# A head of the softmax branches in two steps, and the steps in a new order

## The chip, the cores and the metric

One core of one Trainium2 chip runs the whole kernel in one launch. The metric is the device time of the launch in microseconds (us); of the kernel before three runs are known, 1374.14, 1376.45 and 1376.46 us, so the median is 1376.45 us.

## What is computed

Two blocks follow each other, each with two layers, on 512 tokens of width 1024 (batch 1). A layer projects its input, runs four attention branches of four heads each (head width 64), gates each branch, and projects the result back.

```python
# first block, one layer (abridged)
h = x @ w_in                                   # 9 parts
y_mla = causal_softmax(q_nope|rope(q_pe), k_nope|rope(k_pe), v)   # after two rms norms
y_sb  = stick_breaking(sq, sk, sv)             # sigmoid and suffix sums, no softmax
y_fox = causal_softmax(fq, fk, fv, log_decay=cumsum(log_sigmoid(f)))
y_mem = softmax(q @ mk.T) @ mv                 # 256 memory tokens
merged = sum_n sigmoid(merge_r @ w_merge_up)[n] * ((y_n * silu(gate_n)) @ w_branch[n])
x = layer_norm(alpha * x + merged @ w_out)
# second block, one layer (abridged)
z = rmsnorm(x) @ w_in
o_a = dense softmax (2 key heads, normed and rotated)   # 512 x 512 logits
o_b = window softmax with a sink (3 blocks of 128 keys)
o_c = neighbourhood softmax with a bias table
o_d = two softmaxes, (p0 - lam * p1) @ v, then a norm
x = x + concat(o_n * silu(g_n)) @ w_out
```

## The kernel before

All matmuls work on float32 data that is split into a high and a low part (`split`, L319 a cast on ScalarE, L322 a subtraction on VectorE), and each product is three matmuls: high x high, low x high, high x low (`mm3`, L328 to L330). Matmuls are 128 rows by up to 512 columns. A weight unit (128 x 1024 floats, 512 KB) is loaded by SyncE's queue into `raw` and split into `wh` and `wl`; `w_get` keeps the loads three units ahead of the use (`WP = 3`), in the order that the word lists `WEIGHTS1` and `WEIGHTS2` give.

A softmax head works on four query blocks of 128. For each block two or three matmuls write the logits into a PSUM tile `s` (3 of them in rotation). `softmax` then takes the row maximum on VectorE (L525 with a mask, L528 without) and the exponential with its sum on ScalarE (L534), which writes a tile `p`. When the four tiles `p` are there, `av` transposes them on TensorE, 128 x 128 each, into a PSUM tile `T` (L551, 2 tiles in rotation), splits `T` into `th` and `tl`, and multiplies by V into a PSUM tile `O` (L557, L558, one tile). `o_evac` (L585, L586) brings `O` to SBUF. After the second head of a pair `finish` notes the pair; `do_finish` later repeats the reciprocal sums over the columns by four transposes (`rep`, L626, also a `T` tile) and multiplies on VectorE (L640).

Each branch is a Python generator, and a `yield` ends a step. `weave` takes the steps in the order of a word list: `ORDER1` for the layers of the first block, `ORDER2` for those of the second (a number repeats a word, `f` is one `do_finish`). Projections for the gates (`g`), the stick-breaking heads (`sb`) and the other branches (`mem`, `fox`, `mla`; `a`, `b`, `c`, `d`) are the words. The place in this program order is an instruction's priority: a list scheduler then orders each engine's instructions, taking the earliest that its own plan has ready, so neighbouring steps interleave. After the weave of a first-block layer comes `merge`, after any layer the output projection `w_out`.

Buffers that matter here: `p` has 4, 4, 4 and 2 tiles for the four query blocks in the first block and 2 of each in the second; two PSUM tiles for projections (`proj`, `projv`, `projqr`, `projn` share them), three for `s`, two for `T`, one for `O`. In `mla` the key and value step makes V by two `projv` tiles (L424, taken to SBUF by L414 and L415), then the rotary part of the queries, `projqr` (L968), in the same two tiles.

Of the kernel before, what the change touches and what calls it, by code (L numbers as in the profile page):

```python
# [66 lines left out]
mq:0 mq:1 sb:0 sb:256 gz:6 sbv:0 sbv:1 sbv:2 gz:7 gz:2 gz:3 m:0 m:1 mk:0 mk:1 mv:0 mv:1 sb:128 sb:384 fox:0  # L67
fox:256 cq:0 cq:1 cq:2 gz:4 ckv:0 gz:5 ckv:1 foxv:0 foxv:1 gz:0 fox:128 fox:384 gz:1 kvb qr qb mr mu:0 wb:0
# [3 lines left out]
qa:0 qa:1 ka qd:0 qd:1 kd qc:0 vd g2:6 g2:7 g2:0 g2:1 vab:0 vab:1 g2:2 g2:3 qb2:0 g2:4 kc:0 qb2:1 kb g2:5 vc:0  # L72
# [222 lines left out]
ORDER1 = "first sb g sb g misc sb g2 mem3 fox mem sb2 fox mem mla2 sb g2 mla g mla f fox mla f2 sb fox2 g2 fox g mla f fox mla g fox mla f2 mla f mla3 f"  # L295
ORDER2 = "a d3 c d2 g2 d g2 a g d g f a g b a g f a c b2 a b2 g c g f c d c2 f2 b c f b c f2 w2"
# [14 lines left out]
class Build:  # L311
# [522 lines left out]
    def memory(self, l):  # L834
        self.mem_kv(l)
        yield
        for pr in range(2):
            o, sm = self.new_o(), self.sums()
            for e in range(2):
                h = 2 * pr + e  # L840
                P = []
                for i in range(4):
                    s = self.qk(self.qm[pr][e], self.mks[h], self.mkl[h], i, 0, 256)
                    P.append(self.softmax(i, s, 256, sm[:, e, i : i + 1]))
                self.av(P, [(0, 256)] * 4, lambda j: self.mV[:, j, h], o, e)
# [71 lines left out]
    def mla(self, l):  # L917
# [51 lines left out]
        qr = self.tmp("qr")  # L969
# [6 lines left out]
        for pr in range(2):  # L976
# [14 lines left out]
            for e in range(2):  # L991
                (qa, qb), (ka, kb) = T["q", e], T["k", e]
                P = []
                for i, (_, w) in enumerate(CAUSAL):
# [3 lines left out]
                    P.append(self.softmax(i, s, w, sm[:, e, i : i + 1], self.c["causal"][:, S - w :], sscale=sc))  # L998
                self.av(P, CAUSAL, lambda j: V[pr][:, j, e], o, e)
# [67 lines left out]
    def fox(self, l):  # L1067
# [3 lines left out]
        for pr in range(2):  # L1071
# [10 lines left out]
            for e in range(2):  # L1082
                P = []
                for i, (_, w) in enumerate(CAUSAL):
                    s = self.qk(q[e], ks[e], k2[e], i, 0, w, q2[e], 68)
                    P.append(self.softmax(i, s, w, sm[:, e, i : i + 1], self.c["causal"][:, S - w :]))
                self.av(P, CAUSAL, lambda j: V[pr][:, j, e], o, e)
# [196 lines left out]
    def dense_a(self, l):  # L1284
# [25 lines left out]
        for pr in range(2):  # L1310
            o, sm = self.new_o(), self.sums()
            for e in range(2):
                P = []
                for i in range(4):
                    s = self.qk(raw[pr][e], ks[pr], kl[pr], i, 0, S)
                    P.append(self.softmax(i, s, S, sm[:, e, i : i + 1], sscale=(qsc[:, i, pr, e : e + 1],)))
                self.av(P, DENSE, lambda j: V[0][:, j, pr], o, e)
# [4 lines left out]
    def window_b(self, l):  # L1322
# [15 lines left out]
        for pr in range(2):  # L1338
            o, sm, nm = self.new_o(), self.sums(), self.sums()
            for e in range(2):  # L1340
                P = []
                top = self.nsink[:, l, 2 * pr + e : 2 * pr + e + 1]
                for i, (k0, w) in enumerate(BAND):
                    s = self.qk(q[pr][e], ks[pr], kl[pr], i, k0, w)
                    m = band[:, (128, 0, 0, 0)[i] :][:, :w]
                    P.append(self.softmax(i, s, w, sm[:, e, i : i + 1], m, nm=nm[:, e, i : i + 1], top=top))
                self.av(P, BAND, lambda j: self.vb[:, j, pr], o, e)
# [8 lines left out]
    def diff_d(self, l):  # L1356
# [34 lines left out]
        for pr in range(2):  # L1391
            ku = [unit(hl[2], cols(2 * pr + c, 32), (0, 1, 0, 1)) for c in range(2)]
            o, sm = self.new_o(), self.sums()
            for e in range(2):
                qu = [unit(hl[pr], cols(2 * e + c, 32), (0, 0, 1, 1)) for c in range(2)]
                P = []
                for i in range(4):
# [11 lines left out]
                    P.append(p)  # L1409
                self.av(P, DENSE, lambda j: V[:, j, pr], o, e)  # L1410
# [75 lines left out]
```

## Time and profile before

| | us |
|---|---|
| median of 3 runs | 1376.45 |
| the profiled execution, its own time | 1373.97 |
| its span, first to last instruction | 1372.2 |
| TensorE busy in the span | 1338.4 |
| VectorE busy | 1002.0 |
| ScalarE busy | 816.4 |

The span is 1.8 us shorter than the execution's own time. In the trace the weaves lie at about 15 to 297 us, 410 to 690 us, 803 to 1040 us and 1092 to 1328 us; `merge` follows the first two (to about 345 and 740 us). A matmul's recorded duration is longer than its distance to the next one, since matmuls are pipelined, so a wait that is shorter than that overlap does not show as idle time; the number in brackets at a row's end is idle time and names the instruction that ended it. PEclk is the granted share of TensorE's clock: 1.00 is 2.4 GHz, 0.50 is 1.2 GHz.

### The profile page before, as it was taken

To read this page: it belongs to the slowest core of one execution; us is meant where nothing else is said; L and a number is where in the kernel's file an instruction comes from. 1 tells how busy PE (TensorE), PEld (TensorE's weight loads), DVE (VectorE), ACT (ScalarE), POOL (GpSimd) and SP (SyncE) were. 2 spreads that over 40 slices of the span, in tenths; PEclk is the share of its full clock that TensorE was granted. 3 is DMA by queue.
4 is the path that set the end of the run, shared out by engine and by line. 5 is a ranking of instruction groups with operands and counts; after the bars stand their busy time and mean duration, and the time that the engine had idled before them with its cause. 6 is when DMAs were issued, how large, how long until landed. Compare 5 with 4: busy or idle time off the path is not lost.

```text
span 1372.2 us, 20002 instructions
## 1 busy us (share of the span) xinstructions
PE 1338.4 (98%) x7096; PEld 1099.4 (80%) x7096; DVE 1002.0 (73%) x2075; ACT 816.4 (59%) x1662; POOL 4.3 (0%) x12
## 2 busy tenths in 40 slices
PE   8999999999999999999999999999999999999998
PEld 7887787777789877887777898887877888878776
DVE  6666655998854666476989876788877576888885
ACT  4584556766413755467756344776965446678763
POOL 0000000000000000000000000000000000000000
PEclk9999999999999999999999999999999999999999
DMA  7544223243525434224236345413444265225241
GB/s 232 173 128 106 87 68 93 77 123 114 176 78 152 135 93 137 62 65 108 89 100 190 118 126 153 137 51 104 127 125 156 102 177 154 65 67 146 73 136 70
DMA packets 62419, 160.32 MB, mean 117 GB/s; under 512 B 11184, under 2 KB 11824, under 8 KB 62320
## 3 DMA queue, kind: packets, MB, share of 16 engines
q1 hardware_dynamic: 62320, 159.05, 39.1%
q8 instruction: 56, 0.92, 0.3%
q14 instruction: 43, 0.35, 0.1%
HBM read 117.92 MB, written 8.91 MB: 92 GB/s over the span
## 4 chain that ended last, share of the span: by engine, by line
PE 80%; DVE 8%; ACT 7%; DMA 2%; issue 2%; SPq 0%; DVEq 0%; ACTq 0%
PE proj L328 11%; PE proj L329 11%; PE proj L330 11%; PE T L551 4%; PE pso L330 3%; PE pso L329 3%; PE pso L328 3%; PE O L557 2%; PE O L558 2%; PE projwb L329 2%; PE projwb L328 2%; PE projwb L330 2%; PE s L512 2%; DMA raw<-in_w_dram 2%; PE s L513 2%
## 5 line engine op out<-in xcount | busy, mean ns | idle before, releaser
L328 PE MATMUL proj<-zth,wh 128*128 128x512 f32 (+1 forms) x864 | 322.9, 374 | 7.4 <-ACT wh L319 5.4
L330 PE MATMUL proj<-zth,wl 128*128 128x512 f32 (+1 forms) x864 | 322.7, 374 | 0.0
L329 PE MATMUL proj<-ztl,wh 128*128 128x512 f32 (+1 forms) x864 | 321.9, 373 | 0.3
L322 DVE TENSOR_TENSOR wl<-raw,wh 128x1024 fp32r<-128x1024 f32 (+2 forms) x153 | 182.8, 1195 | 113.3 <-ACT wh L319 111.4
L319 ACT CAST wh<-raw 128x1024 fp32r<-128x1024 f32 (+2 forms) x153 | 157.8, 1031 | 147.5 <-PE proj L329 119.4
L328 PEld LDWEIGHTS proj<-zth,wh 128*128 128x128 f32 x864 | 164.0, 190 | 30.5 <-ACT wh L319 5.4
L330 PEld LDWEIGHTS proj<-zth,wl 128*128 128x128 f32 x864 | 164.0, 190 | 24.7 <-DVE wl L322 1.0
L329 PEld LDWEIGHTS proj<-ztl,wh 128*128 128x128 f32 x864 | 164.2, 190 | 22.8 <-DVE ztl L322 0.8
L322 DVE TENSOR_TENSOR tl<-T,th 128x512 fp32r<-128x512 f32 (+3 forms) x176 | 99.6, 576 | 33.0 <-ACT th L319 31.6
L319 ACT CAST th<-T 128x512 fp32r<-128x512 f32 (+3 forms) x176 | 86.0, 498 | 55.9 <-PE T L551 45.5
L551 PE MATMUL T<-ct,p 128*128 128x128 f32 x560 | 87.3, 275 | 2.7 <-DVE o L640 1.7
L528 DVE TENSOR_REDUCE nm<-s 128x1 f32<-128x512 f32 (+1 forms) x128 | 77.8, 614 | 14.4 <-PE s L513 9.0
L551 PEld LDWEIGHTS T<-ct,p 128*128 128x128 f32 x560 | 66.3, 140 | 19.2 <-DVE o L640 2.6
L534 ACT ACTIVATE p<-s,nm 128x512 f32<-128x512 f32 (+1 forms) x96 | 59.1, 618 | 25.4 <-DVE nm L528 24.9
L557 PE MATMUL O<-tl,V 128*128 128x512 f32 (+3 forms) x160 | 60.0, 376 | 1.5 <-DVE tl L322 1.1
L558 PE MATMUL O<-th,V 128*128 128x512 f32 (+3 forms) x160 | 55.3, 349 | 0.0
L329 PE MATMUL projv<-wl,zth 128*128 128x256 f32 (+1 forms) x192 | 54.7, 285 | 0.0
L328 PE MATMUL projv<-wh,zth 128*128 128x256 f32 (+1 forms) x192 | 54.6, 284 | 0.0
L330 PE MATMUL projv<-wh,ztl 128*128 128x256 f32 (+1 forms) x192 | 54.4, 283 | 0.0
L1107 ACT ACTIVATE sg<-projmu 128x512 f32<-128x512 f32 x64 | 38.1, 598 | 22.7 <-DVE sg L1114 11.6
L330 PE MATMUL projwb<-y,wl 128*128 128x512 f32 x128 | 51.0, 401 | 0.0
L328 PE MATMUL projwb<-y,wh 128*128 128x512 f32 x128 | 51.0, 401 | 0.0
(378 smaller groups left out, 2898.8 us busy)
## 6 DMA issues: line engine op xcount, KB each, us to landing
raw<-in_w_dram SPq DMA_DIRECT2D x173, 512.0 KB, 4.1
xs<-y SPq DMA_DIRECT2D x12, 512.0 KB
ks<-hs SPq DMA_DIRECT2D x32, 128.0 KB, 2.6
early<-xs SPq DMA_DIRECT2D x16, 256.0 KB, 5.1
bias<-in_bias_dram SPq DMA_DIRECT2D x8, 448.0 KB, 4.5
qs<-hs SPq DMA_DIRECT2D x24, 128.0 KB, 3.3
qs<-ls SPq DMA_DIRECT2D x24, 128.0 KB, 2.7
hs<-ls SPq DMA_DIRECT2D x24, 128.0 KB, 2.2
```

The source lines that it names most:

```text
L319: self.nc.scalar.copy(h, src)
L322: self.nc.vector.tensor_tensor(l, src, h, ALU.subtract)
L328: self.nc.tensor.matmul(ps, ah, bh, start=i == 0, stop=False)
L329: self.nc.tensor.matmul(ps, ah, bl, start=False, stop=False)
L330: self.nc.tensor.matmul(ps, al, bh, start=False, stop=i == n - 1)
L512: self.nc.tensor.matmul(s, q[:, cols(i)], k[:, k0 : k0 + w], start=True, stop=False)
L528: nc.vector.tensor_reduce(nm, s, AX.X, ALU.max, negate=True)
L534: nc.scalar.activation(p[:, :w], src, AF.Exp, bias=nm, scale=sc, accum_out=sm)
L551: nc.tensor.transpose(T[:, cols(a)], P[i][:, c : c + 128], self.ident)
L557: nc.tensor.matmul(o, vsel(j), tl[:, :w], start=j == 0, stop=False, skip_group_check=True)
L558: nc.tensor.matmul(o, vsel(j), th[:, :w], start=False, stop=j == nk - 1, skip_group_check=True)
L1107: a = nc.scalar.activation(sg, ps, AF.Sigmoid)
```

## The change

A `yield` is put between the logits-and-exponentials part and the `av` part of a head in all seven softmax branches (in `neigh_c` also one behind the first head), so a head is two steps. `ORDER1`, `ORDER2`, `WEIGHTS1` and `WEIGHTS2` are new lists over the finer steps. No instruction that computes is added or taken away; on every engine the counts by operation, output and shape are equal in both programs.

```diff
-mq:0 mq:1 sb:0 sb:256 gz:6 sbv:0 sbv:1 sbv:2 gz:7 gz:2 gz:3 m:0 m:1 mk:0 mk:1 mv:0 mv:1 sb:128 sb:384 fox:0
+mq:0 mq:1 sb:0 gz:6 sb:256 sbv:0 sbv:1 sbv:2 gz:7 gz:2 gz:3 m:0 m:1 mk:0 mk:1 mv:0 mv:1 sb:128 sb:384 fox:0
...
-ORDER1 = "first sb g sb g misc sb g2 mem3 fox mem sb2 fox mem mla2 sb g2 mla g mla f fox mla f2 sb fox2 g2 fox g mla f fox mla g fox mla f2 mla f mla3 f"
-ORDER2 = "a d3 c d2 g2 d g2 a g d g f a g b a g f a c b2 a b2 g c g f c d c2 f2 b c f b c f2 w2"
+ORDER1 = "first g sb2 misc sb g3 mem6 sb mem sb fox mem g fox sb mem f g mla2 g mla2 fox mla sb f2 fox5 f fox3 g2 mla g mla f mla fox f mla g mla3 f mla4 f"
+ORDER2 = "a d3 c a d2 g2 d2 g d g3 d2 g2 a2 f b a3 b a2 f c b a b g c b2 c d b c2 f c g c2 f d f b3 f c2 b c2 f w c f w"
...
                     P.append(self.softmax(i, s, w, sm[:, e, i : i + 1], self.c["causal"][:, S - w :], sscale=sc))
+                yield
                 self.av(P, CAUSAL, lambda j: V[pr][:, j, e], o, e)
...
+                yield
                 self.av32(P, V[e], O, e)
+                if e == 0:
+                    yield
```

Three places of TensorE's order follow. The first is the key and value step of `mla` in a first-block layer: `projv` makes V, `projqr` takes the PSUM tile of the first `projv`, and `s` are logits of a fox head. Before:

```order
L329 MATMUL projv<-wl,ckh 128x256
L330 MATMUL projv<-wh,ckl 128x256
L512 MATMUL s<-hs 128x128
L513 MATMUL s<-ls 128x128
L512 MATMUL s<-hs 128x256
L513 MATMUL s<-ls 128x256
L328 MATMUL projqr<-cqh,wh 128x512
```

and now, from the end of the first `projv` tile on (the last row is the first of the second tile's twelve; behind those come four more `O` matmuls, then `projqr`):

```order
L330 MATMUL projv<-wh,ckl 128x256
L557 MATMUL O<-tl,V 128x512
L558 MATMUL O<-th,V 128x512
L551 MATMUL T<-ct,p 128x128
L557 MATMUL O<-tl,V 128x384
L558 MATMUL O<-th,V 128x384
L551 MATMUL T<-ct,p 128x128 x2
L328 MATMUL projv<-wh,ckh 128x256
```

The products of a fox head moved between the two tiles of V. The second place is `window_b` in a second-block layer, where the logits of its first head (`s<-ks,hs`) and of its second (`s<-ks,qs`) follow each other. Before:

```order
L512 MATMUL s<-ks,hs 128x384
L513 MATMUL s<-ks,hs 128x384
L512 MATMUL s<-ks,hs 128x256
L513 MATMUL s<-ks,hs 128x256
L512 MATMUL s<-ks,qs 128x256
L513 MATMUL s<-ks,qs 128x256
L512 MATMUL s<-ks,qs 128x384
L1282 MATMUL statd<-ct,sqd 128x2 x4
```

and now:

```order
L513 MATMUL s<-ks,qs 128x256
L328 MATMUL proj<-zth,wh 128x512
L329 MATMUL proj<-ztl,wh 128x512
L330 MATMUL proj<-zth,wl 128x512
L557 MATMUL O<-tl,V 128x512
L558 MATMUL O<-th,V 128x512
L551 MATMUL T<-ct,p 128x128 x2
L557 MATMUL O<-tl,V 128x512
L558 MATMUL O<-th,V 128x512
L551 MATMUL T<-ct,p 128x128 x6
L512 MATMUL s<-ks,qs 128x384
```

Three projection matmuls, four products and eight transposes of another head moved in between the second head's first and second query block. The third place is the first stick-breaking head of a first-block layer; `krt` are four transposes for the rotary keys, and `s` the head's logits. Before, behind a projection:

```order
L328 MATMUL proj<-zth,wh 128x512
L329 MATMUL proj<-ztl,wh 128x512
L330 MATMUL proj<-zth,wl 128x512
L1016 MATMUL krt<-ct,mt 32x128 x4
L890 MATMUL s<-hs 128x128
```

and now, straight behind the stick-breaking values:

```order
L328 MATMUL projv<-wh,zth 128x292
L329 MATMUL projv<-wl,zth 128x292
L330 MATMUL projv<-wh,ztl 128x292
L1018 MATMUL krt<-ct,mt 32x128 x3
L891 MATMUL s<-hs 128x128
```

The logits moved ahead of one projection, so one projection more lies between them and the next matmul of that head.

## Rows read from the trace of the kernel before

**Rows 1.** The page, busy us by engine, share of the span, instructions.

```profile
PE 1338.4 (98%) x7096; PEld 1099.4 (80%) x7096; DVE 1002.0 (73%) x2075; ACT 816.4 (59%) x1662; POOL 4.3 (0%) x12
```

**Rows 2.** Windows of 50 us: length, then busy us of PE, PEld, DVE, ACT, POOL.

```profile
core 0: us, PE busy (x) PEld busy (x) DVE busy (x) ACT busy (x) POOL busy (x), PEclk, DMA share, GB/s
...
200.00:250.00 50.00, 47.77 (x245) 37.66 (x243) 34.83 (x83) 33.95 (x75) 0.00 (x0) 1.00 0.30 84
250.00:300.00 50.00, 48.43 (x256) 37.77 (x256) 47.79 (x122) 39.79 (x90) 0.00 (x0) 1.00 0.32 93
...
600.00:650.00 50.00, 47.41 (x238) 37.42 (x238) 33.42 (x80) 33.01 (x71) 0.00 (x0) 0.97 0.36 96
...
1000.00:1050.00 50.00, 47.84 (x250) 38.65 (x248) 41.16 (x94) 32.67 (x78) 0.00 (x0) 0.97 0.41 122
...
1250.00:1300.00 50.00, 48.05 (x268) 40.18 (x267) 39.90 (x106) 41.53 (x107) 1.05 (x2) 0.97 0.38 104
```

**Rows 3.** Timeline around `projqr`, both layers: start, us, engine, line, idle before.

```profile
231.95 1.28 ACT L614 ACT_TABLE_LOAD   x1
...
234.83 0.65 ACT L414 CAST V<-projv 128x256 fp32r<-128x256 f32 x2
...
235.24 0.76 DVE L415 TENSOR_TENSOR V<-projv,V 128x256 fp32r<-128x256 f32 x2 [0.31 <-ACT V L414]
...
235.80 0.48 PE L328 MATMUL projqr<-cqh,wh 128*128 128x512 f32 x1 [1.37 <-DVE V L415]
...
626.91 0.47 PE L328 MATMUL projqr<-cqh,wh 128*128 128x512 f32 x1 [1.34 <-DVE V L415]
```

**Rows 4.** Timeline of PE behind the second of these waits.

```profile
627.22 0.40 PE L329 MATMUL projqr<-cql,wh 128*128 128x512 f32 x1
627.45 0.40 PE L330 MATMUL projqr<-cqh,wl 128*128 128x512 f32 x1
...
628.56 0.63 PE L328 MATMUL projqr<-cqh,wh 128*128 128x512 f32 x1
628.99 0.63 PE L329 MATMUL projqr<-cql,wh 128*128 128x512 f32 x1
```

**Rows 5.** Timeline of `window_b`, DVE and PE, both layers.

```profile
1002.68 1.22 DVE L322 TENSOR_TENSOR wl<-raw,wh 128x1024 fp32r<-128x1024 f32 x1
...
1004.65 0.62 DVE L525 CUSTOM_DVE_ANT_0 p<-s,band,nsink 128x384 f32<-128x384 f32 x1
...
1003.10 0.28 PE L513 MATMUL s<-ks,qs 128*128 128x256 f32 x1
1005.33 0.44 PE L512 MATMUL s<-ks,qs 128*128 128x384 f32 x1 [1.94 <-DVE sums L525]
...
1292.97 0.45 PE L512 MATMUL s<-ks,qs 128*128 128x384 f32 x1 [1.95 <-DVE sums L525]
```

**Rows 6.** Timeline of the first stick-breaking head, both layers.

```profile
63.50 0.44 PE L907 MATMUL s<-sp,tri 128*128 128x128 f32 x2 [0.57 <-DVE sp L322]
...
452.37 1.21 DVE L322 TENSOR_TENSOR wl<-raw,wh 128x1024 fp32r<-128x1024 f32 x1
...
454.67 0.44 PE L907 MATMUL s<-sp,tri 128*128 128x128 f32 x2 [1.29 <-DVE sp L322]
```

**Rows 7.** Timeline of PE, transposes and products of a fox head behind `projn`.

```profile
243.75 0.33 PE L513 MATMUL s<-kr,qr 68*128 68x384 f32 x1
244.45 0.50 PE L557 MATMUL O<-tl,V 128*128 128x512 f32 x1 [0.37 <-DVE tl L322]
...
245.98 0.27 PE L551 MATMUL T<-ct,p 128*128 128x128 f32 x1
246.44 0.39 PE L557 MATMUL O<-tl,V 128*128 128x256 f32 x1 [0.19 <-DVE tl L322]
```

**Rows 8.** Timeline of PE, transposes that wait for a `T` tile.

```profile
268.14 0.63 PE L551 MATMUL T<-ct,p 128*128 128x128 f32 x4 [0.26 <-DVE o L640]
...
277.06 0.55 PE L551 MATMUL T<-ct,p 128*128 128x128 f32 x3 [0.57 <-DVE o L640]
```

**Rows 9.** TensorE's waits: line, releaser, us in total, times, longest.

```profile
PE proj L328 <- ACT wh L319: 5.4, 1, 5.4
```

More of the change, by code (lines that the diff above doesn't have):

```diff
@@ L66 @@
 WEIGHTS1 = """
-mq:0 mq:1 sb:0 sb:256 gz:6 sbv:0 sbv:1 sbv:2 gz:7 gz:2 gz:3 m:0 m:1 mk:0 mk:1 mv:0 mv:1 sb:128 sb:384 fox:0
-fox:256 cq:0 cq:1 cq:2 gz:4 ckv:0 gz:5 ckv:1 foxv:0 foxv:1 gz:0 fox:128 fox:384 gz:1 kvb qr qb mr mu:0 wb:0
+mq:0 mq:1 sb:0 gz:6 sb:256 sbv:0 sbv:1 sbv:2 gz:7 gz:2 gz:3 m:0 m:1 mk:0 mk:1 mv:0 mv:1 sb:128 sb:384 fox:0
+fox:256 gz:4 cq:0 cq:1 cq:2 gz:5 ckv:0 ckv:1 foxv:0 foxv:1 fox:128 fox:384 gz:0 kvb qr gz:1 qb mr mu:0 wb:0
 wb:1 mu:1 wb:2 wb:3 mu:2 wb:4 wb:5 mu:3 wb:6 wb:7 wo:0 wo:1 wo:2 wo:3 wo:4 wo:5 wo:6 wo:7
@@ L71 @@
 WEIGHTS2 = """
-qa:0 qa:1 ka qd:0 qd:1 kd qc:0 vd g2:6 g2:7 g2:0 g2:1 vab:0 vab:1 g2:2 g2:3 qb2:0 g2:4 kc:0 qb2:1 kb g2:5 vc:0
+qa:0 qa:1 ka qd:0 qd:1 kd qc:0 vab:0 vab:1 vd g2:6 g2:7 g2:0 g2:1 g2:2 g2:3 g2:4 qb2:0 qb2:1 kc:0 kb g2:5 vc:0
 qc:1 kc:1 vc:1 we:0 we:1 wo2:0 wo2:1 wo2:2 wo2:3 wo2:4 wo2:5
@@ L1316, in dense_a @@
                     P.append(self.softmax(i, s, S, sm[:, e, i : i + 1], sscale=(qsc[:, i, pr, e : e + 1],)))
+                yield
                 self.av(P, DENSE, lambda j: V[0][:, j, pr], o, e)
@@ L1346, in window_b @@
                     P.append(self.softmax(i, s, w, sm[:, e, i : i + 1], m, nm=nm[:, e, i : i + 1], top=top))
+                yield
                 self.av(P, BAND, lambda j: self.vb[:, j, pr], o, e)
@@ L1409, in diff_d @@
                     P.append(p)
+                yield
                 self.av(P, DENSE, lambda j: V[:, j, pr], o, e)
@@ L1455, in neigh_c @@
                     P.append(self.softmax(i, s, w, sm[:, e, i : i + 1], bias[:, b0 : b0 + w]))
+                yield
                 self.av32(P, V[e], O, e)
+                if e == 0:
+                    yield
             self.nc.scalar.copy(cr(o), rc(O))
```

## The prediction, made before the changed kernel was run

> **What bounds the kernel now.** I read the page's engine row first: TensorE is busy for 1338.4 of 1372.2 us, VectorE for 1002.0 [rows 1]. TensorE bounds the kernel, and the change gives it the same matmuls; time can come only from its waits and from its clock. The idle time is 1372.2 - 1338.4 = 33.8 us. Then I read the windows of 50 us for two things: where the granted clock is below 1.00 (three windows inside the weaves, at 0.97), and whether another engine is full (VectorE with 47.79 of 50 us at 250 to 300 us, after only 34.83 in the 50 us before) [rows 2]. Last I read the timeline at TensorE's largest waits. They sit where the program order had nothing to put between a result and its use, and they come twice, once in each layer of a block [rows 3, 5 to 8].
>
> **What the clock costs.** Behind the wait of 1.34 us at 626.91 the matmuls of 512 columns start 628.99 - 628.56 = 0.43 us apart, against 627.45 - 627.22 = 0.23 us before [rows 4]: the lower of the two levels, 1.2 against 2.4 GHz. A window at 0.97 lacks 0.03 of 50 us, that is 1.5 us of full clock [rows 2]; by the distances, a stretch at half clock that lacks this much is 3 us long and loses 3 x (1 - 0.23 / 0.43) = 1.4 us. I take 1.5 us for each of the three falls. The equally long wait at 235.80 had no such fall in its window, which stands at 1.00 [rows 2, 3], so a wait of this size takes the clock down in some cases and not in others.
>
> **The change part by part.** Five places, each on TensorE's path.
>
> *A. `projqr`.* It waits for VectorE to take the first V tile out of PSUM, and VectorE waits for ScalarE, which is loading an activation table for 1.28 us and copying gates. Between the second V tile and `projqr` stand only four short matmuls. This costs 1.37 + 1.34 us of idle [rows 3] and one clock fall, 1.5: 4.2 us. Now the products of a fox head stand between the two V tiles and behind the second. The first place of the order shows seven of these rows between the tiles; with the second tile's twelve matmuls (half the columns, so near half of 0.23 us each, 1.4 us) and the products the first tile has about 3 us, where it had under 2. The wait was 1.37 us, so the added 1 us alone would leave a third; but in ScalarE's new order the table load stands behind the casts of V, not ahead of them. Bounds: 0 gained if the wait only shifts, 4.2 if it goes. I take 4.2, since the clock fall needs the long wait.
>
> *B. `window_b`.* The logits of the first head and of the second stand without filler, while only three `s` tiles rotate; the next one waits for a maximum (0.62 us) which is itself late, because VectorE was in a weight split of 1.22 us and another add. Idle 1.94 + 1.95 us [rows 5], and both are in windows at 0.97, so two clock falls, 3.0 us: 6.9 us. In the new order three projection matmuls (0.69 us), four products and eight transposes stand at this point, more than 2 us of TensorE work, and the wait was 1.94. Bounds 0 and 6.9; I take 6.9. If VectorE is late with something else, the cover is gone and the loss returns in full.
>
> *C. The first stick-breaking head.* The matmul with `tri` needs `sp`, which stood on VectorE behind a weight split of 1.21 us; it was late by 0.57 and 1.29 us [rows 6]. Before, 18 projection matmuls stood between the head's logits and `tri`; now 26 stand there, since the projection that came ahead of the logits follows them (the third place of the order). Eight more are 8 x 0.23 = 1.8 us of cover, more than either wait: 1.9 us gained. Bounds 0 and 1.9.
>
> *D. Transposes and products without filler.* From the last logits matmul at 243.75 (384 columns, three quarters of 0.23 us) to the product at 244.45 it is 0.70 us, so 0.53 is lost; at 246.44, behind one transpose of at most 0.1 us, another 0.35 [rows 7]. Twice, for the two layers: 1.8 us, of which the profile shows only 2 x (0.37 + 0.19) as idle. The same fox products now stand beside V (the first place), so I count the 1.8 as gained, bounds 0 and 1.8.
>
> *E. What becomes worse.* `rep` takes one of the two `T` tiles until VectorE has multiplied with it. Before, transposes waited for this 0.26 and 0.57 us in a layer [rows 8]. In the new order I count four places in the kernel where two groups of transposes follow a `rep` with at most two matmuls between, one in `mla` in each first-block layer and one in `window_b` in each second-block layer. At (0.26 + 0.57) / 2 = 0.4 us each this adds 1.7 us; bounds 0 and 4 x 0.57 = 2.3.
>
> *F. What an order does not show.* A to D were chosen because they were the worst. The new order will have a bad place of its own, which depends on how late VectorE and ScalarE run. The nearest row is B: 1.95 + 1.5 = 3.5 us. I take one such place; the bounds are 0 and four of them, 14 us.
>
> At no cost: the weight units and gates that are moved. Their loads follow the same word order as their uses and stay three units ahead, no weight load is among the waits above, and DMA is at 0.41 of its time or less in the windows that I read [rows 2]. The exponentials, splits and `unit` moves of a head are the same in number; their queues are passed in a new order, which is priced with F.
>
> **The sum.** -4.2 - 6.9 - 1.9 - 1.8 + 1.7 + 3.5 = -9.6 us. Against the profiled execution's 1373.97, whose span is 1372.2 and keeps its 1.8 us around it, this is 1364.4 us. That execution lies 2.5 us below the median of the three runs, 1376.45, and just under the fastest, 1374.14; I add half of that distance, so all times below stand against 1375.2. The forecast is 1365.5 us, 0.8% under the median.
>
> **A rule on the clock.** The windows from 200 to 300 us hold many waits of a few tenths and two over half a microsecond, and the clock stays at 1.00 [rows 2, 3, 7, 8]; it fell behind three of the long ones. The Trainium skill ("TensorE: Matmul & The Clock Gate", section "A second HAM failure mode: psum-queue depth-cycling") tells of a kernel that cycled through PSUM banks and whose many micro-idles between groups of matmuls were enough to make the clock go down and up. By that rule the finer interleaving would lose clock where it trades a long wait for many short ones; this trace so far speaks against it, since its finest mixture kept the full clock. The third rival is what it would do here.
>
> **The rivals.**
>
> *1. No change (14%).* VectorE is full at 250 to 300 us, 47.79 of 50 [rows 2]. If that stretch is set by VectorE, cover won before it is only waited for later, in both layers of the first block, and A, C and D come back. B's 6.9 less E and F, 5.2, leaves -1.7 us: 1373.5 us. Against it: TensorE is busy for 48.43 us of that same window, so at most 1.6 us are to be had or lost there by idle time, and VectorE has 15 us free in the window before, where the fox products now go.
>
> *2. Slower: `p` tiles (10%).* A head that is cut holds four `p` tiles from its first step to its second. In the second block there are two of each, and I read from `ORDER2` one point in a layer where three heads are open (`b`, `c`, then `d`). There the third head's maxima and exponentials wait for the first one's transposes, the three `s` tiles stay full, and TensorE runs out of logits. Price: as in B, 3.5 us a place with its clock fall. Two such places, one in each layer, cost 7 and still leave a gain of 2.6. From three places on (9.6 / 3.5 = 2.7) the kernel is slower, from four on by more than can be missed; with six, 21 - 9.6 = +11.4 us: 1386.5 us. For it: the heads are 56, so six is few. Against it: the scheduler lets other work pass, and I find only one such point in a layer.
>
> *3. Slower: the clock (4%).* If many short waits took the clock down in each of the four weaves three times, 12 x 1.5 = 18 us would stand against 9.6 gained: 1383.5 us.
>
> *4. A larger gain (12%).* A to D hold 2.7 + 3.9 + 1.9 + 1.1 = 9.6 us of the 33.8 idle. If the new order also halves the rest, 12 us, and E and F don't come, the gain is 14.8 + 12 = 27 us: 1348 us. For it: cover grows in general when a head is cut. Against it: 5.4 us of the rest is the wait for the first weights, which is not changed [rows 9].
>
> **How the numbers follow.** The forecast holds 60%: a gain of 4 to 18 us, 1357 to 1371 us. A measurement of this kernel tells about 0.2%, 2.8 us, from no change. Faster by more: the forecast and rival 4, 0.60 + 0.12 = 0.72, and I add nothing from the others. Within 0.2%: rival 1, 0.14. Slower: rivals 2 and 3, 0.14. The range for 8 in 10 takes in rival 4, down to 1347, and above, F at its upper bound (10.5 us more) with only a quarter of B gained (5.2 us less): 1381 us.
>
> **What would show it.** Right: no wait over 1 us at `projqr`, at `window_b`'s logits and at the first `tri`; no window of a weave under 1.00; TensorE's idle time near 25 us, with its busy time the same but for the clock. Wrong in A, B or C: the same row still with its wait and its releaser on VectorE. Wrong in F: more than one new wait near 2 us in TensorE's list of waits, and a window at 0.97 behind it. Rival 2: VectorE or ScalarE idle for transposes in the second block. If the clock is at 1.00 throughout and the time is still not below 1371 us, my account of TensorE's waits was wrong as such.

## The result, and the profile after

The changed kernel takes 1360.13 us (median of 4 runs, 1359.7 to 1361.17) against 1376.45 us for the kernel before: a ratio of 0.9882, 95% interval 0.9863 to 0.9901, which is 16.3 us or 1.2% faster. The forecast was 1365.5 us. Part of the 16.3 is the clock: ten runs of the kernel before, timed beside the experiments below, had the mean granted clock that the four of the kernel after had, 0.997 to 0.998, and took 1372.25 to 1374.39 us, about 13 us more than those four. The profiled executions have spans of 1372.2 and 1358.2 us, 14.0 us apart; what follows accounts for these 14.0.

The page's engine row of the kernel after answers to [rows 1]:

```profile
PE 1328.5 (98%) x7096; PEld 1096.4 (81%) x7096; DVE 1000.3 (74%) x2075; ACT 811.3 (60%) x1662; POOL 4.4 (0%) x12
```

The instructions are the same in number. TensorE's idle time went from 33.8 to 1358.2 - 1328.5 = 29.7 us, only 4.1 us less. Its *busy* time fell by 9.9 us for the same 7096 matmuls. So most of the gain stands in time that a list of waits does not show.

TensorE's list of waits after (line, releaser, us in total, times, longest):

```profile
PE proj L328 <- ACT wh L319: 5.6, 1, 5.6
PE projn L328 <- DVE ml L985: 2.6, 2, 1.3
PE pso L328 <- ACT wout L319: 1.7, 2, 1.1
PE s L908 <- DVE sp L322: 1.3, 2, 0.7
...
PE T L551 <- DVE o L640: 1.2, 2, 0.6
PE krt L1018 <- ACT mt L880: 1.1, 2, 0.6
...
PE T L551 <- DVE o L638: 0.6, 2, 0.3
...
PE O L557 <- DVE tl L322: 0.2, 1, 0.2
```

Three of its rows before, for comparison:

```profile
PE T L551 <- DVE o L640: 1.7, 4, 0.6
PE O L557 <- DVE tl L322: 1.1, 4, 0.4
...
PE projn L328 <- DVE ml L984: 0.5, 2, 0.3
```

The waits of `projqr` [rows 3] and of `window_b`'s logits [rows 5] are gone. Three waits are new: `pso` for `wout`, `krt` for `mt`, and `tri` of the second stick-breaking head instead of the first [rows 6]. The wait of `projn` for `ml` has grown from 0.5 to 2.6 us.

The windows of 50 us that answer to [rows 2] (length, busy us of PE, PEld, DVE, ACT, POOL, granted clock, DMA share, GB/s):

```profile
200.00:250.00 50.00, 47.70 (x251) 38.24 (x251) 39.12 (x91) 35.33 (x82) 0.00 (x0) 0.99 0.33 88
250.00:300.00 50.00, 49.50 (x258) 40.06 (x257) 46.67 (x116) 38.53 (x84) 0.00 (x0) 0.98 0.33 95
600.00:650.00 50.00, 47.79 (x263) 38.59 (x262) 41.09 (x98) 35.10 (x80) 0.00 (x0) 1.00 0.31 86
1000.00:1050.00 50.00, 48.59 (x250) 38.59 (x249) 39.05 (x80) 29.67 (x63) 0.00 (x0) 1.00 0.45 142
1250.00:1300.00 50.00, 49.41 (x286) 41.51 (x285) 44.50 (x122) 40.08 (x108) 0.53 (x1) 1.00 0.47 134
```

The three windows that stood at 0.97 before are at 1.00; one stretch across 250 us is new at the low level. Three low-clock stretches inside the weaves have become one. Its beginning, in the timeline of TensorE:

```profile
247.56 0.50 PE L328 MATMUL projn<-ckh,wh 128*128 128x512 f32 x1 [1.30 <-DVE ml L985]
247.90 0.39 PE L329 MATMUL projn<-ckl,wh 128*128 128x512 f32 x1
...
249.97 0.63 PE L329 MATMUL projn<-ckl,wh 128*128 128x512 f32 x1
250.40 0.63 PE L330 MATMUL projn<-ckh,wl 128*128 128x512 f32 x1
```

Behind a wait of 1.30 us the distance goes from 0.23 (the next start is at 248.13) to 250.40 - 249.97 = 0.43 us, as in [rows 4]. And what made `projn` late, in the timeline of ScalarE and VectorE:

```profile
241.96 1.28 ACT L614 ACT_TABLE_LOAD   x1
243.25 0.63 ACT L614 ACTIVATE z<-z 128x512 f32<-128x512 f32 x1
243.79 0.56 ACT L984 CAST mh<-projn 64x512 fp32r<-64x512 f32 x1
244.25 0.63 ACT L614 ACTIVATE z<-z 128x512 f32<-128x512 f32 x1
244.90 1.28 ACT L617 ACT_TABLE_LOAD   x1
246.20 0.58 ACT L984 CAST mh<-projn 64x512 fp32r<-64x512 f32 x1
246.81 0.69 DVE L985 TENSOR_TENSOR ml<-projn,mh 64x512 fp32r<-64x512 f32 x1 [0.43 <-DMA ml<-kr]
```

Between the two copies of `mh` stand a silu and a table load of 1.28 us; another load and another silu stand ahead of the first copy. It is the mechanism of [rows 3] at another place: a table load on ScalarE, a small copy behind it, VectorE behind that, and TensorE at the end.

**Where the 14 us are.** The same matmul was looked up in both traces (the first start of its tile in a layer) and the stretches between compared:

| up to | before | after | gain in the stretch |
|---|---|---|---|
| `projqr`, layer 0 | 235.80 | 232.76 | 3.0 |
| `pso`, layer 0 | 351.58 | 348.66 | -0.1 |
| `projqr`, layer 1 | 626.91 | 620.60 | 3.4 |
| `pso`, layer 1 | 744.19 | 735.70 | 2.2 |
| `pse`, layer 2 | 1017.57 | 1004.92 | 4.2 |
| `pse`, layer 3 | 1305.21 | 1290.06 | 2.5 |
| end | 1372.19 | 1358.21 | -1.2 |

The clock's share can be read from before alone: from `projqr` to the merge's first matmul it takes 277.91 - 235.80 = 42.11 us in layer 0, without a low-clock stretch, and 670.62 - 626.91 = 43.71 in layer 1, with one. A stretch costs 1.6 us by this; two fewer are 3.2. By the distances of the next paragraph, the matmuls inside the three stretches of before lose 1.4, 1.6 and 1.6 us and those inside the one of after 1.5.

**Where it hides in the busy time.** From the starts of all 7096 matmuls I took the distance to the next one, less the usual distance of its shape (0.230 us for 512 columns, 0.174 for 384, 0.118 for 256, 0.109 for 128). What is over, by size:

| us lost | before | after | after, first block whole | first block new | second block new |
|---|---|---|---|---|---|
| over 0.5 us each | 16.2 (16) | 14.0 (16) | 11.7 (11) | 16.2 (17) | 15.7 (18) |
| 0.25 to 0.5 | 15.8 (47) | 12.2 (37) | 17.1 (49) | 9.6 (31) | 19.1 (56) |
| under 0.25, net | 56.3 | 47.9 | 45.7 | 54.0 | 48.2 |
| sum | 88.3 | 74.1 | 74.4 | 79.8 | 83.0 |

The sum falls by 14.2, as the span does. The largest class gives 2.2, the middle one 3.6, and the smallest 8.4, of which 2.8 are the clock: at half clock each distance counts as too long, and of this class 4.0 us lie inside the low-clock stretches of before and 1.2 inside that of after. The other 5.6 us are many gaps below a quarter of a microsecond, which the profile's modelled ends of the matmuls cover. The last three columns are kernels of the next section.

### The profile page after: what moved, and what is told of

Read it like the earlier page. It is cut to its first block, busy times and chain, and to the rows that moved or that the text cites. A ratio compares the mean times of both kernels' runs of the same rounds, so it can differ in the third digit from the quotient of the medians.

```text
span 1358.2 us, 20047 instructions
## 1 busy us (share of the span) xinstructions
PE 1328.5 (98%) x7096; PEld 1096.4 (81%) x7096; DVE 1000.3 (74%) x2075; ACT 811.3 (60%) x1662; POOL 4.4 (0%) x12
## 4 chain that ended last, share of the span: by engine, by line
PE 85%; DVE 6%; ACT 5%; issue 2%; DMA 2%; SPq 0%; DVEq 0%; ACTq 0%
PE proj L329 12%; PE proj L328 12%; PE proj L330 12%; PE T L551 4%; PE pso L330 3%; PE pso L328 3%; PE pso L329 3%; PE O L557 3%; PE O L558 2%; PE projwb L329 2%; PE projwb L330 2%; PE projwb L328 2%; PE s L512 2%; PE s L908 2%; PE projv L329 2%; PE projv L328 2%
## 5 line engine op out<-in xcount | busy, mean ns | idle before, releaser
L322 DVE TENSOR_TENSOR wl<-raw,wh 128x1024 fp32r<-128x1024 f32 (+3 forms) x153 | 182.9, 1196 | 111.3 <-ACT wh L319 109.5
L319 ACT CAST wh<-raw 128x1024 fp32r<-128x1024 f32 (+3 forms) x153 | 157.9, 1032 | 138.2 <-PE proj L329 106.3
L329 PE MATMUL projwb<-y,wh 128*128 128x512 f32 x128 | 51.5, 403 | 0.0
L328 PE MATMUL projwb<-y,wh 128*128 128x512 f32 x128 | 50.9, 398 | 0.0
```

Source lines behind the costliest of these rows:

```text
L319: self.nc.scalar.copy(h, src)
L322: self.nc.vector.tensor_tensor(l, src, h, ALU.subtract)
L328: self.nc.tensor.matmul(ps, ah, bh, start=i == 0, stop=False)
L329: self.nc.tensor.matmul(ps, ah, bl, start=False, stop=False)
```

## The experiments

Each ratio is against the kernel before on the same chip, and a gain in us is the ratio's share of 1376.45 us, except where two medians are subtracted; the kernel after stands at 0.9882 [0.9863, 0.9901].

**Each block alone.** The first kernel takes the words, the weight order and the cut of the first block alone, the second those of the second block.

```diff
-ORDER1 = "first sb g sb g misc sb g2 mem3 fox ...
+ORDER1 = "first g sb2 misc sb g3 mem6 sb mem ...
...
+                yield
```

> Only the first block changes (cut heads in memory, mla and fox, the new ORDER1 and WEIGHTS1); the second block is that of the kernel before. My theory (the gain is the sum of the waits that went at A, C and D, with one clock fall less and one more): the first pso of the second layer came 8.5 us earlier in the trace, so this kernel gains 8 to 9 us, 1367 to 1368 us, and keeps the two 1.9 us waits at window_b's logits with their two clock falls. Rival (every cut head gives its share): 24 of 56 heads are in this block, 24/56 of 16.3 us is 7.0 us, 1369.5 us.

> Only the second block changes (cut heads in dense_a, window_b, diff_d and neigh_c, the new ORDER2 and WEIGHTS2). My theory: from the second layer's pso to the end the trace gained 14.0 - 8.5 = 5.5 us, so 1370 to 1372 us, with no clock fall behind 700 us and the projqr waits of 1.3 to 1.4 us still there. Rival (every cut head gives its share): 32 of 56 heads, 9.3 us, 1367 us. The two gains of this run and of the one with the first block must add up to the whole one, 14 to 16 us, within 2 us; if not, what one block does changes the other.

Measured: first block 1366.26 us, 0.9934 [0.9918, 0.9951], 9.1 us faster; second block 1370.07, 0.9958 [0.9944, 0.9972], 5.8 us faster. Together 14.9 of 16.3: the two add up, and the first gives more. The table of sizes tells what each is: the first block's gain is in the gaps of 0.25 to 0.5 us (47 to 31 of them), while its largest class stays at 16.2, new long waits for old ones. The second block's gain is in the smallest class, which the clock moves. In that run no window of the weaves was below 1.00, although the first block's `projqr` still waited, 1.45 us in layer 0 and 1.07 in layer 1:

```profile
600.00:650.00 50.00, 47.40 (x247) 37.40 (x246) 34.89 (x83) 34.32 (x77) 0.00 (x0) 1.00 0.36 96
```

So 1.5 of its 5.8 us (the stretch from `projqr` to the merge in layer 1, which it did not change) is one low-clock stretch that did not happen. All three stretches of before are absent, and they had lost 4.6 us, nearly all of the 5.3 us by which this kernel's sum is smaller. The runs give the clock a smaller share: at a granted clock of 0.996 to 0.997 three runs of this kernel took 1369.90 to 1370.87 us and five of the kernel before on the same chip 1372.55 to 1375.45, some 4 us apart. So apart from the clock the second block gave between 1 and 4 us.

**Whole heads in the new order.** The new order with no head cut: the seven `yield`s behind the logits are taken out, and a whole head stands where its second step stood.

```diff
-ORDER2 = "a d3 c a d2 g2 d2 g d g3 d2 g2 a2 f b a3 b ...
+ORDER2 = "a d3 c a d g2 d g d g3 d g2 a f b a b ...
...
-                yield
```

> The heads are whole again (the seven yields inside heads are taken out; the one between the heads of neigh_c stays), and each stands where its second step stands in the new ORDER1 and ORDER2; the projections, gates and finishes keep their new places. My theory (the filler at the places is what counts, and most of it are steps that are moved): A, B and C keep their filler, D and some of the small waits come back; 60 to 80% of the gain stays, 1364 to 1368 us, no 1.9 us wait at window_b. Rival (the cut itself gives the gain): 20% or less stays, 1373 to 1376 us.

Measured: 1411.72 us, 1.0260 [1.0242, 1.0278], 36 us *slower*. Theory and rival were both wrong. At the first block's end it was still 7.0 us ahead of before (after: 8.5); everything was lost in the second. Its waits, and its stretch from the first `pse` to the first `pso` of layer 2, then the same stretch of after:

```profile
PE s L512 <- ACT p L534: 9.4, 11, 1.7
PE pso L328 <- ACT wout L319: 9.0, 2, 4.5
...
PE s L1400 <- ACT p L534: 4.0, 6, 1.1
```

```profile
1003.86:1056.05 52.19, 41.97 (x212) 31.26 (x212) 41.70 (x108) 32.64 (x85) 0.00 (x0) 0.97 0.27 80
```

```profile
1004.92:1030.99 26.07, 25.64 (x141) 20.52 (x141) 20.59 (x50) 17.96 (x43) 0.00 (x0) 1.00 0.14 52
```

The logits of a whole head stand without filler, so the next ones wait until the exponentials free an `s` tile (17 waits), and work that had filled gaps earlier is left for the end of the layer: 212 matmuls in place of 141 there, 10.2 us idle in 52.2, at a lower clock. Over the whole kernel the low-clock stretches ahead of its end lose 11.7 us by the distances, against 1.5 in the kernel after.

**Whole heads in the first block only.** To see whether that reading of the blocks holds:

```diff
-ORDER1 = "first g sb2 misc sb g3 mem6 sb mem sb fox mem g ...
+ORDER1 = "first g sb2 misc sb g3 mem3 sb mem sb fox g ...
...
-                yield
```

> The kernel after, with the heads of the first block (mem, fox, mla) whole again, each at the place of its second step; the second block stays cut. Theory from the run with all heads whole: the first block hardly needs the cut, and all of the loss of 36 us + 16 us came from the second block. So 1.5 us over after, 1360 to 1363. Rival: the cut gives cover in both blocks, and the first block's good number in that run was made by less pressure further on; then +5 us or more, 1365 or over.

Measured: 1360.02 us, 0.9883 [0.9864, 0.9903]: the same as after. It does have fewer and longer waits: `projn` now waits 1.9 us in each of the two layers. The profiled run had one low-clock stretch in the weaves, behind the second of these waits and not behind the first, which stands at 247 us:

```profile
200.00:250.00 50.00, 47.14 (x251) 38.13 (x249) 37.72 (x86) 34.06 (x76) 0.00 (x0) 1.00 0.33 88
...
600.00:650.00 50.00, 47.65 (x258) 38.54 (x256) 38.80 (x95) 35.44 (x78) 0.00 (x0) 0.97 0.33 88
```

So in the first block the cut is worth nothing and the order of the words everything. The two kernels with whole heads differ only in the second block: there the cut is worth 1411.72 - 1360.02 = 51.7 us *in this order* (on two chips, where the kernel before took 1375.65 and 1376.25 us). The cut by itself should be worth nothing there either: with each head word doubled in the old order the program order would be that of before (argued; this was not run). That another order of whole heads would do as well was not tried.

**The last `window_b` wait moved, nothing else.** In the kernel before, one word of the second order changes places, so that something stands between the two heads of `window_b`.

```diff
-... f2 b c f b c f2 w2"
+... f2 b c f c b f2 w2"
```

> The kernel before with one swap in ORDER2: near the end 'b c f b c f2' becomes 'b c f c b f2', so the last window head comes behind the last neighbourhood pair, and its logits no longer follow those of the head before at once. Nothing else. My theory of B: the two waits of 1.94 and 1.95 us go with their two clock falls (2 x 1.5), 6.9 us less what the moved filler costs at the very end of the weave, where the last head then has less beside it (up to 2 us a layer): 1370 to 1373 us. Rival (VectorE is the limit there, the wait only moves): 1375 to 1378 us, and a wait of 1.5 us or more on VectorE within 20 us of the old place.

Measured: 1382.46 us, 1.0050 [1.0033, 1.0068], 6.8 us slower. The wait stood at the same time with another name, and the list has a second one, of `pse` for VectorE, 1.9 us in each layer:

```profile
1006.80 1.05 PE L1282 MATMUL statd<-ct,sqd 128*128 128x2 f32 x8 [2.19 <-ACT sqd L1413]
```

It was 1.94 us for VectorE before [rows 5]; now it is 2.19 for ScalarE. Here reordering without filler moved a wait; the new order put matmuls there that need neither engine. The swap also leaves the last head with nothing beside it at the weave's end, which is where `pse` waits, so this run does not test the wait of `window_b` alone.

**`projqr` alone.** In the kernel before, `projqr` gets a PSUM tile of the `s` group, so that it does not need the one that VectorE still copies V out of.

```diff
-        ps = self.psp.tile([128, S], F32, tag="proj", name="projqr")
+        ps = self.pss.tile([128, S], F32, tag="S", name="projqr")
```

> The kernel before, with the one projection projqr put into a PSUM tile of the s group in place of the proj group, which was still held by the first V tile; the order of the words stays. Theory (term A of the prediction): projqr no longer waits for VectorE to copy that V tile; 2.7 us of waits in two layers and the one low-clock stretch behind it go: -3 to -4.2 us, about 1372. Rival: the wait only moves to the next thing that needs the late ScalarE and VectorE (the next proj tile, or the logits that lose their s tile), 0 to -1 us.

Measured: 1377.57 us, 1.0011 [0.9995, 1.0027]: no gain, the rival. The wait of `projqr` is gone from the list; in its place stand, before all,

```profile
PE T L551 <- ACT p L534: 3.0, 6, 0.9
PE O L557 <- DVE tl L322: 2.4, 6, 0.5
```

and the stretch from `projqr` to the first `pso` grew. The stretch in both layers, of before, then of this kernel:

```profile
235.80:351.58 115.78, 113.43 (x535) 88.12 (x535) 105.31 (x211) 81.29 (x157) 0.00 (x0) 1.00 0.37 110
626.91:744.19 117.28, 114.90 (x536) 89.39 (x536) 105.44 (x211) 81.47 (x157) 0.00 (x0) 0.99 0.37 108
```

```profile
235.24:355.87 120.63, 115.14 (x541) 90.13 (x540) 107.63 (x214) 83.55 (x163) 0.00 (x0) 0.99 0.37 109
629.66:748.87 119.21, 113.68 (x541) 89.04 (x540) 107.58 (x214) 83.65 (x163) 0.00 (x0) 1.00 0.37 110
```

The new low-clock stretch in layer 0, 0.99 in its row, has no wait of a microsecond ahead of it. Within 3 us stand three short ones, and behind the last the rows start 0.43 us apart (281.55, 281.98):

```profile
278.84 0.55 PE L551 MATMUL T<-ct,p 128*128 128x128 f32 x3 [0.29 <-DVE o L640]
279.90 0.47 PE L328 MATMUL projwb<-y,wh 128*128 128x512 f32 x1 [0.52 <-issue]
281.03 0.73 PE L328 MATMUL projmu<-mr,wh 128*128 128x512 f32 x1 [0.65 <-ACT mr L319]
```

One caution: `projqr` now holds one of the three `s` tiles, which may itself delay logits, so the run does not show what the wait alone would give.

**The grown `projn` wait.** In the kernel after, the silu, which already is issued behind `gate_copy`, is held behind the copy of `mh` as well, so that no table load stands between the copies.

```diff
-                    nc.scalar.copy(a[0:64], ps[half(e)])
+                    mh = nc.scalar.copy(a[0:64], ps[half(e)])
+                    if pr:
+                        self.gate_copy = mh
...
-... mla g mla3 f mla4 f"
+... mla4 g f mla4 f"
```

> The kernel after, with the last silu of the gates held until ScalarE has issued the second pair's copy of mh (a dependence between the two), and that gate step one place later in the order. Theory: the new wait of projn (2.6 us in two layers, and the low clock behind the first, 1.5 us) comes from the two table loads of 1.28 us that stand between the two mh copies on ScalarE. With the loads moved behind them the wait goes: 4.1 us at most, 2 us at least, so 1356 to 1358 against the 1360.1 of the kernel after on this measure. Rival 1: the projn wait is set by VectorE (the subtraction ml itself, or what stands ahead of it); then projn still waits about 1.3 us a layer and the time is the same. Rival 2: the loads only delay the exponentials that follow and a wait of the same size appears at the transposes behind, 0 to -1 us.

Measured: 1362.95 us, 0.9901 [0.9882, 0.9921]; the intervals of the ratios overlap, but there is no gain of 2 to 4 us: each of the six runs, 1361.84 to 1364.36 us, is slower than each of the four of the kernel after, 1359.70 to 1361.17, though its granted clock was as high or higher (0.997 to 0.999). The cause was right in the main: one table load, not two, stood between the copies, and with the loads moved the wait is gone and the clock stayed at full. But a wait of `O` for `tl` came:

```profile
PE O L557 <- DVE tl L322: 2.9, 5, 1.1
```

From `projqr` to `pso` it takes 116.52 and 116.77 us where after takes 115.90, with its low-clock stretch, and 115.10:

```profile
232.76:348.66 115.90, 113.51 (x530) 90.23 (x530) 101.99 (x193) 78.94 (x143) 0.00 (x0) 0.99 0.38 114
620.60:735.70 115.10, 112.71 (x530) 88.86 (x530) 102.04 (x193) 78.96 (x143) 0.00 (x0) 1.00 0.38 115
```

```profile
232.96:349.48 116.52, 113.65 (x530) 88.73 (x530) 102.18 (x193) 80.06 (x143) 0.00 (x0) 1.00 0.38 113
621.20:737.97 116.77, 114.05 (x529) 89.02 (x530) 102.38 (x193) 79.73 (x143) 0.00 (x0) 1.00 0.39 113
```

The same matmuls (530), one long wait fewer, and 0.6 and 1.7 us longer; the low-clock stretch of after in the first of them, 1.5 us, hides that both lost about 2. With `krt` moved as well:

```diff
-ORDER1 = "first g sb2 misc sb g3 ...
+ORDER1 = "first g sb3 misc g3 ...
```

> As the run before, and in addition the three stick-breaking head steps at the start stand together ahead of misc and the three gate steps, so that the krt matmul of misc follows later. Theory: krt's new wait for ScalarE's mt (1.1 us in two layers) goes, and nothing else changes: 1 us under the run before, 1355 to 1357. Rival: the stick head's own wait (the second tri for sp, 1.3 us) grows since the matmuls of misc no longer cover it: the same as the run before or up to 1.3 us slower.

Measured: 1380.85 us, 1.0041 [1.0027, 1.0055], some 18 us slower than the run before it. `krt`'s wait went, but the order of the weights was left as it was, and the weights of `mem` came late:

```profile
PE projmk L328 <- ACT mh L319: 8.8, 2, 8.5
```

The two profiles are 23.3 us apart. The wait accounts for 8.8 of them; three low-clock stretches, which the run before it has none of, lose 6.1 by the distances; and new waits of `s` for a DMA make 2.5. The rest is not assigned. A word's place and its weights' place are one edit.

**The stick-breaking head alone.** The kernel before, with the first words of after.

```diff
-mq:0 mq:1 sb:0 sb:256 gz:6 ...
+mq:0 mq:1 sb:0 gz:6 sb:256 ...
...
-ORDER1 = "first sb g sb g misc sb g2 mem3 ...
+ORDER1 = "first g sb2 misc sb g3 mem3 ...
```

> The kernel before, with only the first words of the first block ordered as in the kernel after (gate step ahead of two stick-breaking steps, then misc, one more, three gates) and the three weight units that go with them. Theory (term C): the first tri no longer waits for sp (1.9 us in two layers), and krt's wait for mt appears as in the kernel after (1.1 us): -0.8 us in sum, between -2 and +0.5. Rival: the first block's gain in the kernel after begins here already, -2.9 us at the layer's output; then -3 to -6 us.

Measured: 1375.72 us, 0.9988 [0.9975, 1.0001], -1.7 us with an interval of -3.4 to +0.1. `tri`'s wait is gone, `krt`'s 1.1 us is there. It agrees with the theory's -0.8, though not clear of no change at all, and leaves no room for most of the first block's gain here.

**Is it VectorE?** With single waits giving nothing from `projqr` to `pso`, the next theory was the first rival's: VectorE, nearly full at 250 to 300 us [rows 2], holds that stretch. The splits of sixteen weight units of a layer were put on POOL, in after and in before.

```diff
-        self.nc.vector.tensor_tensor(l, src, h, ALU.subtract)
+        (leng or self.nc.vector).tensor_tensor(l, src, h, ALU.subtract)
...
-                    self.split(*(t[:, c] for t in parts[0]), raw[:, c])
+                    self.split(*(t[:, c] for t in parts[0]), raw[:, c], leng=nc.gpsimd if key[0] in ("kvb", "qr", "qb", "mr", "mu", "wb") else None)
```

> The kernel after, with the splits (raw minus wh) of the sixteen weight units kvb, qr, qb, mr, mu and wb of each first-block layer on POOL in place of VectorE; nothing else changes. Theory: in both kernels the stretch from projqr to the first pso (some 115 us a layer) is held by VectorE, which is 93 to 98% busy in the worst 60 us of before; that is why taking single waits out of it gained nothing. With some 15 splits of 1.2 us, 18 us of VectorE work a layer, gone, the queue of VectorE is short, and most of TensorE's lost time there goes: 2 to 5 us a layer, so -4 to -10 us against the kernel after (1350 to 1356). Rival 1: TensorE's stalls there come from the order and from ScalarE, and VectorE's load does not matter: within 2 us of after. Rival 2: POOL is so much slower at a split that weights come late, or it slows VectorE beside it: slower than after, with waits of proj for DVE or POOL wl in the list.

> The same edit in the kernel before. Theory (VectorE holds the stretch): the wait of projqr for V (2.7 us) and the waits for nm, ml, tl and o in the 40 us behind go or halve: -5 to -12 us against before, at least as much as in the kernel after, since before has more to lose there. Rival (the order holds it): the wait of projqr goes only in part, since V waits for ScalarE's table load; -3 to 0. Rival 2 (POOL too slow): slower, as above.

Measured: 1386.32 us, 1.0073 [1.0055, 1.0092], and 1391.71, 1.0118 [1.0097, 1.0138]: both slower, by the second rival. The costs in the first (count, busy us, mean ns of one, idle before), then the same VectorE groups of after, from 220 to 360 us:

```profile
L322 POOL TENSOR_TENSOR wl<-raw,wh 128x1024 fp32r<-128x1024 f32 x28 | 72.3, 2590 | 375.0 <-ACT wh L319 363.6 <-PE s L330 6.9 <-PE projmu L330 4.5
...
L1117 DVE TENSOR_TENSOR sg<-sg 128x512 f32<-128x512 f32 x21 | 21.1, 1005 | 0.5
L1113 DVE TENSOR_TENSOR sg<-projwb,sg 128x512 f32<-128x512 f32 x29 | 19.9, 687 | 8.9 <-PE projwb L330 7.3 <-ACT zth L319 1.4
```

```profile
L1113 DVE TENSOR_TENSOR sg<-projwb,sg 128x512 f32<-128x512 f32 x32 | 21.7, 684 | 3.2 <-PE projwb L330 3.1
...
L1117 DVE TENSOR_TENSOR sg<-sg 128x512 f32<-128x512 f32 x24 | 16.5, 686 | 0.3
```

A split costs 2.59 us there against 1.22 on VectorE, `projwb` waits for it (8.9 us in 6 waits), and VectorE's additions of two SBUF tiles go from 0.69 to 1.00 us, while its products with a PSUM tile stay at 0.69. The Trainium skill ("GPSIMD Engine Reference", section "Specifications") says the two engines contend where a VectorE instruction has two SBUF inputs; the two groups agree with it. So this pair did not test the theory. The last run takes the splits away instead; TensorE reads the high half in place of the low one, so the low halves of these weights are missing from its products:

```diff
-                if key[0] != "m":
+                if key[0] in LIGHT:
+                    nc.scalar.copy(parts[0][0][:, c], raw[:, c])
+                elif key[0] != "m":
```

> The kernel before, with the splits of the weight units kvb, qr, qb, mr, mu and wb in the first block left out: no low half is computed for them, and TensorE reads the high half in its place, so it does the same matmuls and VectorE does some 18 us less in each first-block layer, with nothing put on POOL. Theory (VectorE's load sets the stretch from projqr to the first pso, 115.8 us in layer 0 of before with its clock at 1.00, 117.3 in layer 1 with a low-clock stretch): both shorten by 2 to 5 us, the whole by 5 to 11: 1365 to 1371 against 1376. Rival 1 (the order sets it, whatever VectorE's load): the same waits stand there, the stretch stays within 1 us and the whole within 2 us of before. Either way the wait of projqr itself should stay in part, since V waits for ScalarE's table load.

Measured: 1372.19 us, 0.9987 [0.9969, 1.0004], -1.8 us. VectorE works 94 instead of 105 us in the stretch, and the stretch is 1.3 and 1.7 us shorter:

```profile
235.31:349.81 114.50, 113.29 (x540) 89.30 (x540) 94.19 (x200) 82.43 (x159) 0.00 (x0) 1.00 0.39 118
625.75:741.34 115.59, 114.61 (x540) 90.69 (x540) 94.35 (x200) 82.18 (x159) 0.00 (x0) 0.99 0.38 117
```

The theory asked for 2 to 5 us a layer: it fell. Nor is it VectorE that `projqr` waits for: the wait grew from 2.7 to 4.2 us with VectorE idle for 7.20 us ahead of taking V, which ScalarE's table load at 231.45 us held up:

```profile
233.67 0.76 DVE L420 TENSOR_TENSOR V<-projv,V 128x256 fp32r<-128x256 f32 x2 [7.20 <-ACT V L419]
```

In the second block, which is the same here as before, the wait of `window_b` is there with 1.94 us, and no low-clock stretch follows it, in this layer or the next (the windows at 1000 and 1250 us are at 1.00). VectorE's load has a part in the stretch, and a small one. What sets the stretch's length at some 114 to 116 us is open: it has 113 us of busy TensorE and gives little back, whichever wait is taken out.

## Why the prediction was right, and where it was not

The sign was right and the forecast 5.4 us too high, inside its own range of a gain of 4 to 18 us (by its own terms the sum is 1365.6; the 0.1 is rounding). That it came so near is in part luck. Of the 9.6 us of its sum, 3.0 are the clock, and some 3 came. The other 6.6 are waits; the gaps over half a microsecond gave 2.2, and smaller gaps, which the sum counts at one place only, gave the other 9. Term by term:

- *A, `projqr` (-4.2).* The row is right: both waits and the clock stretch are gone. As a price it is not shown: the run that took the wait out gave nothing, though it took an `s` tile as well. That the wait and its clock loss could be added to the sum as if the time behind them stood still is the step that failed.
- *B, `window_b` (-6.9).* 3.9 us of waits and two low-clock stretches are gone, 7.1 by rows. The second block alone gave 5.8, of which 1.5 belongs to the first block's clock, and apart from all clock between 1 and 4, so the waits did not add up as priced here either; and 1.2 was lost again at the end of the kernel, where the last `pso` waits 1.1 us for `wout`, which the prediction did not name. That filler and not mere distance was needed fits the run with the moved word, which changed the weave's end as well and so does not show it alone.
- *C, `tri` (-1.9).* The wait went, but `krt` (1.1) and the second head's `tri` (1.3) took its place. The prediction counted the cover of the first head and not who lost it.
- *D (-1.8).* The waits of `O` for `tl` fell from 1.1 to 0.2 us in the list. The idea that a gap is longer than its idle row was right, and the term far too small: it was counted at one place a layer, and this class, gaps under half a microsecond, gave 3.6 + 8.4 - 2.8 = 9.2 us of the 14.2, the clock left out.
- *E (+1.7).* Waits of `T` for `o` are 1.8 us, as against 1.7 before. The new places came and the old ones [rows 8] went; the term should have been a difference.
- *F (+3.5).* One bad place, `projn`, in both layers, with one clock stretch: 2.6 + 1.6 = 4.2. Right in kind and size; `krt` and `pso` came on top.

*The expected view.* "Idle time near 25 us, busy time the same but for the clock" was wrong: 29.7, and 9.9 us less busy. The prediction took a busy TensorE for a working one. Nor were all windows of the weaves at 1.00: the stretch across 250 us is at 0.99 and 0.98.

*The rivals.* The first, that cover won in the first block is only waited for later, describes the stretch from `projqr` to `pso` (-0.1 and 2.2 us, or 1.4 and 0.7 with the two low-clock stretches of 1.5 taken out, and two repaired waits that gave nothing) but its cause, VectorE, accounts for 1.3 to 1.7 us a layer, and the block's gain stands mostly ahead of `projqr` (3.0 and 3.4 us in the two layers), where the rival saw VectorE with time to spare. The second rival, three open heads short of `p` tiles, did not come: TensorE's list after has no wait for `p`. Such waits came with *whole* heads, at the `s` tiles. The third, the clock, did not come: the finer order had one low-clock stretch inside the weaves for three, and the rule on many short idles of the Trainium skill ("TensorE: Matmul & The Clock Gate", section "A second HAM failure mode: psum-queue depth-cycling") was not borne out by the kernel after. One run bears it out in small: with `projqr` in an `s` tile the clock fell behind waits of 0.29, 0.52 and 0.65 us. The fourth, a larger gain, is where the missing 4 us belong: the small gaps shrank in general. Which words of the new order shrank them was not tested.

## What to carry to other kernels

Price a reordering by all gaps between the bottleneck engine's starts, by size, and not by the top of its list of waits: here the few worst places traded one for one, and the gain was in gaps that the profile counts as busy. Taking out one wait by itself proves little: in both trials here the time did not fall, and other waits for the same engines came a few microseconds later. The new order put filler there that needs neither late engine; that this is what helps is argued from the orders and not tested alone. And test a cut and an order apart, block by block: in the new order the cut was worth nothing in one block and 51.7 us in the other. Last, compare runs at the same granted clock before a difference of 2 or 3 us is explained.

## What the runs showed of the hardware

- A wait does not settle the clock. `projqr` waited 1.37 and 1.34 us before [rows 3], and only the second was followed by the low level; the second-block kernel waited 1.45 without a fall. `projn` waited 1.30 us in both layers of the kernel after and 1.90 in both with whole first-block heads, each time with a fall in one layer only. `window_b`'s logits waited 1.94 and 1.95 us before [rows 5] with a fall behind both, and 1.94 twice in the kernel without the splits, with none. With `projqr` in an `s` tile the low level came behind waits of 0.29, 0.52 and 0.65 us within 3 us, without a longer one. A stretch costs 1.4 to 1.6 us when it comes, so a profile of one execution decides by chance over 1 to 3 us here, and on one chip the runs of the kernel before went from 1371.74 us at a mean granted clock of 0.999 to 1381.74 at 0.992.
- POOL's two-input split of 128x1024 took 2.59 us, and VectorE's own two-input SBUF operations in the same stretch took almost half as long again, 1005 in place of 686 ns.
